# Two projections of the second block begun together, token-major, with seven held pieces

## The chip, the core and the metric

The kernel runs on one core of one Trainium2 chip. The time is the device time of one execution in microseconds. Five engines work in parallel, each through its own queue in order: TensorE (PE; its weight loads are shown as PEld), VectorE (DVE), ScalarE (ACT), GpSimd (POOL) and SyncE (SP), which issues the DMA transfers.

## The reference

Two transformer blocks on 256 tokens of width 1024 in float32. The first block (pool mixer, stick-breaking attention, cross-attention, dense feed-forward) is left as it is. The second one, cut to what matters:

```python
h = rms_norm(x, g_mix)
qa, ka, va, qb, kb, vb, qi, ki, wi, ga, gb = jnp.split(h @ w_in, SPLIT_POINTS, axis=-1)
qa = rope(heads(qa)); ka = rope(heads(ka)); qb = rope(heads(qb)); kb = rope(heads(kb))
qi = rope(qi.reshape(b, s, IDX_HEADS, IDX_DIM)); ki = rope(ki); wi = wi * IDX_SCALE
o_a = moba_attend(qa, ka, va)
o_b = dsa_attend(qb, kb, vb, qi, ki, wi)     # keys chosen by index scores:
#   score = einsum('qh,qhs->qs', wi, relu(einsum('qhd,sd->qhs', qi, ki)));  top 64 of them
mixed = sigmoid(ga) * (o_a @ w_proj_a) + sigmoid(gb) * (o_b @ w_proj_b)
x = x + mixed @ w_out
x = x + hier_moe(rms_norm(x, g_ffn), ...)    # 32 experts, two for each token
return rms_norm(x, g_final)
```

## The kernel before

A float32 product is made of three passes. `split_to` (L153) writes a high part with an ACT copy (whi, xhi; L155) and a low part with a subtraction on DVE, or on POOL where told so (wlo, xlo; L156). `mm3` (L185 to L187) then multiplies high by high, low by high and high by low into one accumulator.

Weights come by `wload` (L147) in chunks of 1 MB on SP's queue. A `piece` (L164) is half a chunk, split, 2 k-tiles of 512 columns. Its home is taken in turn from `homes`: for the projections discussed here either the usual pool (`base`, three buffers) or the pool `px2` (three buffers for each part). A projection of 512 columns has four pieces; for each token tile (two tiles of 128 tokens) a piece gives 6 matmuls of 512 columns, so a projection has 48. `ts_pair` (L219) forms pieces and multiplies each with token tile 0 and then 1; with `hold=4` it collects four pieces and then does all of tile 0 before tile 1.

The second block begins where the dense feed-forward ends. For each token tile `post_norm_add` (L305) adds the normalized feed-forward output to x (L312, L315), and `normed_T` (L285) normalizes x: ACT sums the squares (sqscr, L272), DVE adds them (rsm, L282), POOL takes the power (rsr, L284), DVE multiplies (ntok: L290 by the gain, L294 by rsr, L296 for the second half), PE transposes (xtp, L301), and the result is split to xhi and xlo. Tile 1 runs through this while PE already multiplies tile 0.

The first projection is qiT, the queries of the index scores, with four held pieces (L662), two of its low parts on POOL. `rope_heads` (L644) rotates a projection for each tile: three DVE products (L637, L638, L640; rr and r), an addition on POOL (L642), four transposes on PE (rt, L656) and a copy by ACT. After it come the index keys and weights (kiwi, 72 columns), the index scores (il, L702; DVE adds them up, L707), and on DVE the top-k of them (L712, L713), 16 steps. Then the projections qTb, kTb, vb of the attention "b" that uses that top-k, and qTa, kTa, va of "a". `attend` (L720) makes scores (as, L732), a masked maximum (L739), the exponentials on ACT (L746), the normalization (L752), the transposes of the probabilities (L756) and their product with v (ao, L765) to oah, oal, obh, obl. Last come gates (256-column matmuls, ACT's tanh into tg), the products y of the attention outputs (`merge`, L492; 24 matmuls each; DVE multiplies tg by y, L508), wo, the routing, and from L1117 the experts, whose weights (8 chunks of room) stream from HBM.

The order of the instructions on each engine isn't that of the code: a scheduler sets it when the program is built, within the pools' buffers and dependences. `issue_after` holds a split behind another one.

```python
qiT = rope_heads(3072, 1.0, "qiT", at, 4, first[0], 2, (1,3))
...
for name, c0, pool in (("b", 1536, atb), ("a", 0, at)):
    qT = rope_heads(c0, 0.125, "qT" + name, pool)
```

Of the kernel before, what the change touches and what calls it, by code (L numbers as in the profile page):

```python
# [9 lines left out]
F32 = mybir.dt.float32  # L10
# [8 lines left out]
P = 128  # L19
S = 256  # L20
D = 1024
NT = S // P
# [59 lines left out]
def block_kernel(ctx: ExitStack, tc: tile.TileContext, A, out: bass.AP):  # L82
    nc = tc.nc
# [134 lines left out]
    def ts_mm(dst, pcs, act, tt):  # L218
        for k0, per, pc in pcs:  # L219
            for j in range(per):  # L220
                mm3(dst, cut(act, k0 + j, tt), (pc[0][:, j, :], pc[1][:, j, :]), k0 + j == 0, k0 + j == KT - 1)

    def ts_pair(src, c0, n, act, name, hold=1, after=(), free=0, aside=()):
        o = acc_tile(name)
        kk = 2048 // n
        per = kk // 2
        group, npc, made = [], KT // per, 0
        for c in range(KT // kk):
            w = wload(rows(src, c * kk * P, kk, c0, n), kk, n)
            for h in range(2):  # L230
                group.append((c * kk + h * per, per, piece(w[:, h * per:(h + 1) * per, :], per, n,
                                                           after if made >= free else (),
                                                           nc.gpsimd if made in aside else None)))
                made += 1
                if len(group) == hold or made == npc:
                    for tt in range(NT):
                        ts_mm(o[tt][:, :n], group, act, tt)
                    group = []
                    hold = 1
        return o  # L240
# [375 lines left out]
    tmp = s2.enter_context(tc.tile_pool(name="at2t", bufs=2, side="right", reuse_waits="tile"))  # L616
    s1 = ExitStack()
    px = s1.enter_context(tc.tile_pool(name="px2", bufs=1, side="left", reuse_waits="tile"))
    homes.update(list=[base, (px, 3)], i=0)
    slots_of.update(list=[(ring, 4)], i=0)  # L620
    g_pre = gain_row(A["g_mix_2"][0])
    xt = xt_tiles()
# [18 lines left out]
                                in1=stab[:, tt, None, 32:64].to_broadcast([P, nh, 32]), op=ALU.mult)  # L641
        nc.gpsimd.tensor_tensor(out=dst, in0=t1, in1=t2, op=ALU.add)  # L642

    def rope_heads(c0, scale, name, pool, *how):  # L644
        o = ts_pair(w2in, c0, 512, xt, name, *how)
        if how:
            nc.sync.dma_start(out=cs2[:, 0:256], in_=A["c2"][:, 384:640])
            nc.sync.dma_start(out=cneg, in_=A["c2"][:, 0:384])
        dst = pool.tile([P, 4, S], F32, name=name, tag="qk", bufs=2)
        for tt in range(NT):  # L650
            r = rop.tile([P, 8, 64], F32, name="rr", tag="rr")
            rope_to(r, o[tt].rearrange("p (h d) -> p h d", h=8), tt, 8)
            b = m_tile("rt")
            rf = r.rearrange("p h d -> p (h d)")
            for c in range(4):
                nc.tensor.transpose(b[:, c * P:(c + 1) * P], rf[:, c * P:(c + 1) * P], ident)  # L656
            nc.scalar.activation(dst[:, :, tt * P:(tt + 1) * P], b.rearrange("p (c t) -> p c t", c=4), AF.Copy,
                                 scale=scale)
        return dst


    qiT = rope_heads(3072, 1.0, "qiT", at, 4, first[0], 2, (1,3))  # L662
    s1.close()
    homes.update(list=[base], i=0)
    s1 = ExitStack()
# [31 lines left out]
    def index_scores():  # L697
        for h in range(8):
            ks = slice((h % 2) * 64, (h % 2) * 64 + 64)
            b = m_tile("il")  # L700
            for tt, a0, a1 in SPANS:
                nc.tensor.matmul(b[:, a0:a1], lhsT=qiT[ks, h // 2, tt * P:(tt + 1) * P], rhs=kiT[ks, 0:a1 - a0],  # L702
                                 start=True, stop=True, skip_group_check=True)
            r = tmp.tile([P, 384], F32, name="irl", tag="ap", bufs=4)
            nc.scalar.activation(r, b[:, :384], AF.Relu)
            for tt, a0, a1 in SPANS:
                nc.vector.scalar_tensor_tensor(out=score[:, a0:a1], in0=r[:, a0:a1], scalar=wi[:, tt, h:h + 1],  # L707
                                               in1=(cneg if h == 0 else score)[:, a0:a1], op0=ALU.mult, op1=ALU.add)
        for tt, a0, a1 in SPANS:
            for _ in range(TOPK // 8):  # L710
                m8 = tmp.tile([P, 8], F32, name="m8", tag="m8")
                nc.vector.max(out=m8, in_=score[:, a0:a1])  # L712
                nc.vector.match_replace(out=score[:, a0:a1], in_to_replace=m8, in_values=score[:, a0:a1],  # L713
                                        imm_value=GONE)
        nc.vector.tensor_scalar(out=sbias, in0=score, scalar1=-2.9e38, scalar2=NEG, op0=ALU.is_gt, op1=ALU.mult)
        nc.vector.tensor_tensor(out=sbias, in0=sbias, in1=cneg, op=ALU.add)

    index_scores()

    def attend(qT, kT, v, bias, name):  # L720
# [48 lines left out]

    qkv = {}  # L770
    for name, c0, pool in (("b", 1536, atb), ("a", 0, at)):
        qT = rope_heads(c0, 0.125, "qT" + name, pool)
        kT = rope_heads(c0 + 512, 1.0, "kT" + name, pool)
        o = ts_pair(w2in, c0 + 1024, 512, xt, "v" + name)
        v = pool.tile([P, NT, 512], F32, name="v" + name)
        for tt in range(NT):
            nc.vector.tensor_copy(v[:, tt, :], o[tt])
        qkv[name] = (qT, kT, v)
# [457 lines left out]
```

## Time and profile before

| | us |
|---|---|
| runs | 1096.18, 1099.05, 1097.20 |
| median | 1097.2 |
| the profiled execution's time | 1095.6 |
| its span | 1093.9 |
| around the span | 1.7 |
| PE busy | 946.4 (87%) |
| DVE busy | 447.5 (41%) |
| ACT busy | 354.4 (32%) |
| POOL busy | 52.9 (5%) |

Mean granted clock of TensorE: 0.931. The span is the profiled execution from first to last instruction; the profiled time is the whole execution's. In a timeline a row gives the start, the duration, engine, line, operation and in brackets how long the engine had been idle before and what released it. Matmuls overlap, so a row's duration is longer than the distance between two starts.

### The profile page before, as it was taken

The numbers are of one execution on the slowest core, as the hardware profiler recorded it, in microseconds if no ns is written. First come the engines' busy times: TensorE is split into PE (matmuls) and PEld (weight loads), VectorE is DVE, ScalarE is ACT, GpSimd is POOL, SyncE is SP. The second block draws the span as 40 slices with busy tenths as digits, with TensorE's granted clock in tenths as the row PEclk, the third lists the DMA queues.
The fourth block names the chain that finished last, engine by engine and source line by source line (L and its number), as shares of the span: only waits on it lengthen the run. The fifth ranks groups of instructions, "written<-read, shape, count | busy, mean of one in ns | idle before, by whom it ended". The sixth has DMA issues, their size and how long they took to land.

```text
span 1093.9 us, 14757 instructions
## 1 busy us (share of the span) xinstructions
PE 946.4 (87%) x6119; PEld 653.5 (60%) x6119; DVE 447.5 (41%) x750; ACT 354.4 (32%) x552; POOL 52.9 (5%) x45
## 2 busy tenths in 40 slices
PE   6999999999999998999999999775776767667665
PEld 5989988978899996878889974222121212112101
DVE  5555536666545556679664751110101000011102
ACT  4555655555444444444655431000000000000002
POOL 1000012120000002211000000000000000000000
PEclk9999999999999999999999999887888877887879
DMA  9844347567555533645546789999999999999996
GB/s 330 276 157 155 116 135 251 194 238 262 191 192 190 165 101 112 228 153 181 166 171 238 305 302 420 419 419 422 416 421 417 418 416 421 418 419 420 417 422 269
DMA packets 109800, 310.76 MB, mean 284 GB/s; under 512 B 11040, under 2 KB 58144, under 8 KB 89376
## 3 DMA queue, kind: packets, MB, share of 16 engines
q1 hardware_dynamic: 109728, 309.77, 74.8%
q8 instruction: 49, 0.80, 0.3%
q14 instruction: 23, 0.19, 0.0%
HBM read 308.70 MB, written 1.05 MB: 283 GB/s over the span
## 4 chain that ended last, share of the span: by engine, by line
PE 57%; DMA 37%; DVE 3%; ACT 1%; issue 1%; SPq 1%; POOL 0%; POOLq 0%; ACTq 0%; DVEq 0%
DMA wchunk<-in_experts_dram 36%; PE gate L185 4%; PE gu L186 4%; PE gu L185 4%; PE gu L187 4%; PE gate L187 4%; PE gate L186 4%; PE hb L1117 2%; PE fo L185 2%; PE fo L187 2%; PE fo L186 2%; PE y L185 1%; PE y L187 1%; PE y L186 1%; PE wo L185 1%; PE wo L186 1%
## 5 line engine op out<-in xcount | busy, mean ns | idle before, releaser
L156 DVE TENSOR_TENSOR wlo<-wchunk,whi 128x1024 fp32r<-128x1024 f32 (+1 forms) x180 | 222.9, 1240 | 157.3 <-ACT whi L155 154.7
L155 ACT ACTIVATE whi<-wchunk 128x1024 fp32r<-128x1024 f32 (+1 forms) x193 | 200.8, 1048 | 223.7 <-PE gu L186 55.8
L1117 PE MATMUL hb<-wchunk,xs 128*32 128x512 f32 x1016 | 162.6, 739 | 80.5 <-DMA wchunk<-in_experts_dram 75.1
L1117 PEld LDWEIGHTS hb<-wchunk,xs 128*32 128x32 f32 x1016 | 25.9, 120 | 198.4 <-DMA wchunk<-in_experts_dram 156.4
L1117 PE MATMUL yb<-wchunk,mw 128*32 128x512 f32 (+1 forms) x544 | 71.6, 639 | 24.5 <-DMA wchunk<-in_experts_dram 21.8
L185 PE MATMUL gate<-xhi,whi 128*128 128x256 f32 x320 | 92.1, 288 | 0.6 <-DVE tg L508 0.6
L186 PE MATMUL gate<-xlo,whi 128*128 128x256 f32 x320 | 91.5, 286 | 0.0
L187 PE MATMUL gate<-xhi,wlo 128*128 128x256 f32 x320 | 91.4, 286 | 0.0
L187 PE MATMUL gu<-xhi,wlo 128*128 128x256 f32 x288 | 81.4, 283 | 0.0
L186 PE MATMUL gu<-xlo,whi 128*128 128x256 f32 x288 | 81.2, 282 | 0.0
L185 PE MATMUL gu<-xhi,whi 128*128 128x256 f32 x288 | 81.2, 282 | 0.0
L1181 DVE TENSOR_TENSOR x<-x,comb 128x512 f32<-128x512 f32 (+1 forms) x34 | 22.3, 656 | 126.6 <-PE comb L1179 126.6
L185 PEld LDWEIGHTS gate<-xhi,whi 128*128 128x128 f32 x320 | 61.2, 191 | 3.3 <-issue 2.4
L186 PEld LDWEIGHTS gate<-xlo,whi 128*128 128x128 f32 x320 | 61.2, 191 | 1.4 <-issue 1.3
L187 PEld LDWEIGHTS gate<-xhi,wlo 128*128 128x128 f32 x320 | 61.1, 191 | 1.4 <-issue 1.4
L1117 PEld LDWEIGHTS yb<-wchunk,mw 128*32 128x32 f32 x544 | 14.3, 117 | 76.5 <-DMA wchunk<-in_experts_dram 46.5
L1144 ACT ACTIVATE mw<-hT 128x512 f32<-128x512 f32 x8 | 4.8, 597 | 167.4 <-PE hT L1142 167.4
L987 DVE TENSOR_TENSOR xs<-gat,gk 128x512 f32<-128x512 f32 x16 | 11.1, 692 | 115.7 <-PE gat L979 115.7
L185 PEld LDWEIGHTS gu<-xhi,whi 128*128 128x128 f32 x288 | 55.1, 191 | 0.3
L186 PEld LDWEIGHTS gu<-xlo,whi 128*128 128x128 f32 x288 | 54.9, 191 | 0.3
L187 PEld LDWEIGHTS gu<-xhi,wlo 128*128 128x128 f32 x288 | 54.8, 190 | 0.0
L1139 DVE TENSOR_TENSOR mw<-hb,ms 128x512 f32<-128x512 f32 x8 | 5.5, 692 | 106.2 <-PE hb L1117 106.2
(395 smaller groups left out, 1687.8 us busy)
## 6 DMA issues: line engine op xcount, KB each, us to landing
wchunk<-in_experts_dram SPq DMA_DIRECT2D x187, 1024.0 KB, 19.9
wchunk<-in_w_in_dram SPq DMA_DIRECT2D x43, 1024.0 KB, 5.3
wchunk<-in_w_ffn_in_dram SPq DMA_DIRECT2D x22, 1024.0 KB, 5.2
wchunk<-in_w_ffn_out_dram SPq DMA_DIRECT2D x11, 1024.0 KB, 5.0
wchunk<-in_w_out_dram SPq DMA_DIRECT2D x8, 1024.0 KB, 5.8
wchunk<-in_experts_dram SPq DMA_DIRECT2D x8, 512.0 KB, 14.4
wchunk<-in_w_mem_kv_dram SPq DMA_DIRECT2D x2, 1024.0 KB, 6.8
wchunk<-in_w_pool_o_dram SPq DMA_DIRECT2D x2, 1024.0 KB, 5.3
```

The costliest lines, as they stand in the source:

```text
L155: a = nc.scalar.activation(hi, src, AF.Copy)
L156: return a, (eng or nc.vector).tensor_tensor(out=lo, in0=src, in1=hi.bitcast(F32), op=ALU.subtract)
L185: nc.tensor.matmul(o, lhsT=lh[0], rhs=rh[0], start=start, stop=False)
L186: nc.tensor.matmul(o, lhsT=lh[0], rhs=rh[1], start=False, stop=False)
L187: return nc.tensor.matmul(o, lhsT=lh[1], rhs=rh[0], start=False, stop=stop)
L987: nc.vector.tensor_tensor(out=xss[g][:, ks, :], in0=b.rearrange("p (k t) -> p k t", k=4), in1=gk[:, ks, None].to_broadcast([P, 4, P]), op= ...
L1117: nc.tensor.matmul(o[ps, :].rearrange("p (h n) -> p h n", h=m), lhsT=lhsT[:, ps], rhs=w[e], start=first, stop=last, skip_group_check=True, ...
L1139: nc.vector.tensor_tensor(out=h, in0=hb[1], in1=s, op=ALU.mult)
L1144: nc.scalar.activation(mw[:, 1, :], b, AF.Copy)
L1181: nc.vector.tensor_tensor(out=xa, in0=xa, in1=cb[:, :n], op=ALU.add)
```

## The change

qiT and qTb are projected together. Their eight pieces are formed up front; qiT's four and three of qTb's are held (seven), for which px2 gets a fourth buffer. Token tile 0 is multiplied with qiT's pieces and three of qTb's, then tile 1 with qiT's, then the fourth of qTb's with tile 0 and all of them with tile 1. The rope of qiT follows, that of qTb stands before the index scores; the loop over "b" and "a" takes this qTb.

```diff
--- before.py
+++ after.py
@@ -616,7 +616,7 @@
     tmp = s2.enter_context(tc.tile_pool(name="at2t", bufs=2, side="right", reuse_waits="tile"))
     s1 = ExitStack()
     px = s1.enter_context(tc.tile_pool(name="px2", bufs=1, side="left", reuse_waits="tile"))
-    homes.update(list=[base, (px, 3)], i=0)
+    homes.update(list=[base, (px, 4)], i=0)
     slots_of.update(list=[(ring, 4)], i=0)
     g_pre = gain_row(A["g_mix_2"][0])
     xt = xt_tiles()
@@ -641,11 +641,8 @@
                                 in1=stab[:, tt, None, 32:64].to_broadcast([P, nh, 32]), op=ALU.mult)
         nc.gpsimd.tensor_tensor(out=dst, in0=t1, in1=t2, op=ALU.add)
 
-    def rope_heads(c0, scale, name, pool, *how):
-        o = ts_pair(w2in, c0, 512, xt, name, *how)
-        if how:
-            nc.sync.dma_start(out=cs2[:, 0:256], in_=A["c2"][:, 384:640])
-            nc.sync.dma_start(out=cneg, in_=A["c2"][:, 0:384])
+    def rope_heads(c0, scale, name, pool, o=None):
+        o = o or ts_pair(w2in, c0, 512, xt, name)
         dst = pool.tile([P, 4, S], F32, name=name, tag="qk", bufs=2)
         for tt in range(NT):
             r = rop.tile([P, 8, 64], F32, name="rr", tag="rr")
@@ -659,7 +656,20 @@
         return dst
 
 
-    qiT = rope_heads(3072, 1.0, "qiT", at, 4, first[0], 2, (1,3))
+    qp = ts_pieces(w2in, 3072, 512, first[0], 2, (1, 3))
+    bp = ts_pieces(w2in, 1536, 512, first[0], 0, ())
+    nc.sync.dma_start(out=cs2[:, 0:256], in_=A["c2"][:, 384:640])
+    nc.sync.dma_start(out=cneg, in_=A["c2"][:, 0:384])
+    qo, bo = {}, {}
+    for tt in range(NT):
+        for o, n in ((qo, "qiT"), (bo, "qTb")):
+            o[tt] = acc1.tile([P, 512], F32, name=n, tag="acc", bufs=4)
+        ts_mm(qo[tt], qp, xt, tt)
+        if tt == 0:
+            ts_mm(bo[0], bp[:3], xt, 0)
+    ts_mm(bo[0], bp[3:], xt, 0)
+    ts_mm(bo[1], bp, xt, 1)
+    qiT = rope_heads(3072, 1.0, "qiT", at, qo)
     s1.close()
     homes.update(list=[base], i=0)
     s1 = ExitStack()
@@ -715,6 +725,7 @@
         nc.vector.tensor_scalar(out=sbias, in0=score, scalar1=-2.9e38, scalar2=NEG, op0=ALU.is_gt, op1=ALU.mult)
         nc.vector.tensor_tensor(out=sbias, in0=sbias, in1=cneg, op=ALU.add)
 
+    qTb = rope_heads(1536, 0.125, "qTb", atb, bo)
     index_scores()
 
     def attend(qT, kT, v, bias, name):
@@ -769,7 +780,7 @@
 
     qkv = {}
     for name, c0, pool in (("b", 1536, atb), ("a", 0, at)):
-        qT = rope_heads(c0, 0.125, "qT" + name, pool)
+        qT = qTb if name == "b" else rope_heads(c0, 0.125, "qT" + name, pool)
         kT = rope_heads(c0 + 512, 1.0, "kT" + name, pool)
         o = ts_pair(w2in, c0 + 1024, 512, xt, "v" + name)
         v = pool.tile([P, NT, 512], F32, name="v" + name)
```

The new order of the instructions around the second norm, with buffer numbers. On PE, at the end of tile 0 (qiT's first accumulator is 4117 before and 4157 now, its second 4118 and 4201; qTb's are 4158 and 4202), before:

```order
L185 MATMUL qiT_4117<-whi_4134,xhi_4031 128x512
L186 MATMUL qiT_4117<-wlo_4135,xhi_4031 128x512
L187 MATMUL qiT_4117<-whi_4134,xlo_4032 128x512
L301 MATMUL xtp_4100<-ck_86,ntok_4088 128x128 x4
L301 MATMUL xtp_4108<-ck_86,ntok_4088 128x128 x4
L185 MATMUL qiT_4118<-whi_4121,xhi_4031 128x512
L186 MATMUL qiT_4118<-wlo_4122,xhi_4031 128x512
```

and now:

```order
L186 MATMUL qTb_4158<-wlo_4149,xhi_4031 128x512
L187 MATMUL qTb_4158<-whi_4148,xlo_4032 128x512
L185 MATMUL qTb_4158<-whi_4148,xhi_4031 128x512
L186 MATMUL qTb_4158<-wlo_4149,xhi_4031 128x512
L187 MATMUL qTb_4158<-whi_4148,xlo_4032 128x512
L301 MATMUL xtp_4100<-ck_86,ntok_4088 128x128 x4
L301 MATMUL xtp_4108<-ck_86,ntok_4088 128x128 x4
L185 MATMUL qiT_4201<-whi_4119,xhi_4031 128x512
L186 MATMUL qiT_4201<-wlo_4120,xhi_4031 128x512
L185 MATMUL qTb_4202<-whi_4138,xhi_4031 128x512
L186 MATMUL qTb_4202<-wlo_4139,xhi_4031 128x512
L187 MATMUL qiT_4201<-whi_4119,xlo_4032 128x512
```

Between qiT's last matmul of tile 0 and the transposes stand 18 matmuls of qTb now, of which the last are shown, and the first low pass (L187) of tile 1 comes after two of qTb's.

On DVE, from the residual addition of tile 1 (L315) on, before:

```order
L315 SCALAR_TENSOR_TENSOR x<-pn,rsr,x 128x512 x2
L290 TENSOR_TENSOR ntok<-x,grow 128x512
L282 TENSOR_SCALAR rsm<-ss 128x1
L294 TENSOR_SCALAR ntok<-ntok,rsr 128x512
L296 SCALAR_TENSOR_TENSOR ntok<-x,rsr,grow 128x512
L637 TENSOR_TENSOR rr<-qiT,cs_4116 128x512
L638 TENSOR_TENSOR r_4190<-qiT,cs_4116 128x8x32
L640 TENSOR_TENSOR r_4190<-qiT,cs_4116 128x8x32
```

and now:

```order
L315 SCALAR_TENSOR_TENSOR x<-pn,rsr,x 128x512 x2
L156 TENSOR_TENSOR wlo<-wchunk,whi 128x1024
L290 TENSOR_TENSOR ntok<-x,grow 128x512
L156 TENSOR_TENSOR wlo<-wchunk,whi 128x1024 x2
L637 TENSOR_TENSOR rr<-qiT,cs_4116 128x512
L638 TENSOR_TENSOR r_4259<-qiT,cs_4116 128x8x32
L640 TENSOR_TENSOR r_4259<-qiT,cs_4116 128x8x32
L282 TENSOR_SCALAR rsm<-ss 128x1
L294 TENSOR_SCALAR ntok<-ntok,rsr 128x512
L296 SCALAR_TENSOR_TENSOR ntok<-x,rsr,grow 128x512
```

Three weight splits and the rope of qiT's tile 0 (L637 to L640) moved ahead of rsm; L294 and L296, before the rope until now, come after it.

On POOL, in the same place, before:

```order
L284 TENSOR_TENSOR rsr<-rsm,half 128x1
L156 TENSOR_TENSOR wlo<-wchunk,whi 128x1024
L284 TENSOR_TENSOR rsr<-rsm,half 128x1
L642 TENSOR_TENSOR rr<-rr,r_4190 128x512
L642 TENSOR_TENSOR rr<-rr,r_4202 128x512
```

and now:

```order
L284 TENSOR_TENSOR rsr<-rsm,half 128x1
L156 TENSOR_TENSOR wlo<-wchunk,whi 128x1024
L642 TENSOR_TENSOR rr<-rr,r_4259 128x512
L284 TENSOR_TENSOR rsr<-rsm,half 128x1
L642 TENSOR_TENSOR rr<-rr,r_4271 128x512
```

The rope's addition (L642) went ahead of rsr (L284) of the second tile.

On PE at the end of the gates (y_5773 before is the first y; now y_5804 and y_5774 are under way together with the last product ao of attention "a"), the semaphore waits written behind the rows, before:

```order
L186 MATMUL y_5802<-obl_4903,whi_5799 128x256
L187 MATMUL y_5802<-obh_4902,wlo_5770 128x256
L185 MATMUL y_5835<-oah_5076,whi_5831 128x256 [waits DVE_49]
L186 MATMUL y_5835<-oal_5077,whi_5831 128x256
L187 MATMUL y_5835<-oah_5076,wlo_5832 128x256
```

and now:

```order
L776 MATMUL ao_5245<-apts_5243,va_4901 64x128
L186 MATMUL y_5804<-obl_4905,whi_5800 128x256
L187 MATMUL y_5804<-obh_4904,wlo_5801 128x256
L185 MATMUL y_5774<-oah_5078,whi_5771 128x256 [waits Activation_49]
L185 MATMUL y_5836<-oah_5078,whi_5833 128x256 [waits DVE_49]
L186 MATMUL y_5836<-oal_5079,whi_5833 128x256
```

The y that waits for DVE now stands one matmul behind the end of y_5804; before, y_5835 with the same kind of wait stood one whole y (y_5802) behind the end of y_5773.

## Rows read from the trace of the kernel before

**Rows 1.** The chain in order of time, 640 to 700 us: start us, us, what

```profile
652.53 13.87 PE hb L1117 x128
...
682.36 20.09 DMA wchunk<-in_experts_dram
```

**Rows 2.** Busy time by stretch: PE, PEld, DVE, ACT, POOL, granted clock, DMA share, GB/s

```profile
640.00:650.00 10.00, 9.27 (x80) 8.62 (x79) 6.81 (x45) 6.38 (x15) 1.09 (x2) 1.00 0.94 352
650.00:660.00 10.00, 10.00 (x95) 4.67 (x97) 2.41 (x10) 0.36 (x1) 0.00 (x0) 1.00 0.67 251
```

**Rows 3.** The chain in order of time: one 512-column and one 256-column matmul

```profile
438.29 0.23 PE qiT L186
...
590.20 0.12 PE gate L187
```

**Rows 4.** Timeline of PE, 432 to 438 us: start, us, engine, line, operation

```profile
432.48 0.40 PE L187 MATMUL qiT<-whi,xlo 128*128 128x512 f32 x1
435.13 1.29 PE L301 MATMUL xtp<-ck,ntok 128*128 128x128 f32 x8 [2.25 <-DVE ntok L294]
436.45 0.50 PE L185 MATMUL qiT<-whi,xhi 128*128 128x512 f32 x1
436.78 0.40 PE L186 MATMUL qiT<-wlo,xhi 128*128 128x512 f32 x1
437.56 0.50 PE L187 MATMUL qiT<-whi,xlo 128*128 128x512 f32 x1 [0.39 <-DVE xlo L156]
```

**Rows 5.** Timeline of DVE, 427 to 437 us

```profile
427.90 1.24 DVE L156 TENSOR_TENSOR wlo<-wchunk,whi 128x1024 fp32r<-128x1024 f32 x1
429.07 3.54 DVE L315 SCALAR_TENSOR_TENSOR x<-pn,rsr,x 128x512 f32<-128x512 f32 x2
432.53 0.68 DVE L290 TENSOR_TENSOR ntok<-x,grow 128x512 f32<-128x512 f32 x1
433.56 0.21 DVE L282 TENSOR_SCALAR rsm<-ss 128x1 f32<-128x1 f32 x1 [0.34 <-ACT sqscr L272]
434.50 0.49 DVE L294 TENSOR_SCALAR ntok<-ntok,rsr 128x512 f32<-128x512 f32 x1 [0.73 <-POOL rsr L284]
...
435.56 0.68 DVE L637 TENSOR_TENSOR rr<-qiT,cs 128x512 f32<-128x512 f32 x1
...
436.83 1.28 DVE L156 TENSOR_TENSOR xlo<-xtp,xhi 128x512 fp32r<-128x512 f32 x2
```

**Rows 6.** Timeline of DVE: the same addition for token tile 0

```profile
418.63 1.42 DVE L315 SCALAR_TENSOR_TENSOR x<-pn,rsr,x 128x512 f32<-128x512 f32 x2
```

**Rows 7.** Timeline of POOL, 428 to 437 us and 499 us

```profile
428.90 2.50 POOL L156 TENSOR_TENSOR wlo<-wchunk,whi 128x1024 fp32r<-128x1024 f32 x1 [0.47 <-ACT whi L155]
433.92 0.55 POOL L284 TENSOR_TENSOR rsr<-rsm,half 128x1 f32<-128x1 f32 x1 [2.52 <-DVE rsm L282]
436.99 1.28 POOL L642 TENSOR_TENSOR rr<-rr,r 128x512 f32<-128x512 f32 x1 [2.52 <-DVE r L640]
...
499.36 1.30 POOL L642 TENSOR_TENSOR rr<-rr,r 128x512 f32<-128x512 f32 x1 [0.22 <-DVE r L640]
```

**Rows 8.** Timeline of DVE, from the first top-k step to the first softmax

```profile
482.86 0.29 DVE L712 MAX8 m<-score 128x8 f32<-128x128 f32 x1
...
499.63 2.11 DVE L156 TENSOR_TENSOR wlo<-wchunk,whi 128x1024 fp32r<-128x1024 f32 x1
...
519.95 0.29 DVE L739 CUSTOM_DVE_ANT_0 ap<-as,score 128x128 f32<-128x128 f32 x1 [0.15 <-DVE score L716]
...
524.20 1.01 DVE L752 TENSOR_SCALAR ap<-ap,arc 128x128 f32<-128x128 f32 x4
```

**Rows 9.** Timeline of PE: the first transposes of probabilities

```profile
527.21 0.33 PE L756 MATMUL as<-ck,ap 128*128 128x128 f32 x1
```

**Rows 10.** Timeline of PE and of DVE: the end of the first y

```profile
598.67 0.28 PE L187 MATMUL y<-oah,wlo 128*128 128x256 f32 x1
...
599.00 0.69 DVE L508 SCALAR_TENSOR_TENSOR tg<-tg,y 128x512 f32<-128x512 f32 x1 [0.69 <-PE y L187]
```

## The prediction

> **What bounds the kernel now.** I read the chain of the work that ended last first, in order of time: it is on PE up to 682.36 us and then runs in 20-us steps of expert loads nearly to the end [rows 1]. That DMA stage does not hide what is lost before it. In 640 to 650 us the DMA engines are 0.94 busy and in 650 to 660 only 0.67, since all expert slots are full and the queue waits for the first expert matmul (hb, at 652.53 us) to free them [rows 1, 2]. So a microsecond by which PE reaches hb sooner or later moves the slots, the loads behind them and the end by a microsecond. I price the change on PE's time up to 652 us, one to one.
>
> From the start of the second block's projections (426 us) to 640 us PE is packed: a 512-column matmul starts every 0.23 us, a 256-column one every 0.12 [rows 3]. There are two openings where the change works [rows 4]. After the last qiT matmul of token tile 0 (432.48 us) the transposes of tile 1's normalized tokens come only at 435.13, with 2.25 us idle, released by the ntok write of VectorE. And the first L187 of tile 1 waits 0.39 us more for xlo. Counted by starts these are 435.13 - 432.48 - 0.23 = 2.42 us and (437.56 - 436.78) - 0.23 = 0.55 us. Together 2.97 us is all that more work in this place can win. The measurement of this kernel can tell about 0.3%, 3.3 us, from no change; the full gain would be below that.
>
> **Why tile 1's tokens are late.** On DVE the residual add L315 takes 3.54 us for two halves, 429.07 to 432.61, where the same pair for tile 0 took 1.42 [rows 5, 6]; a 2.50-us weight split runs on POOL from 428.90 to 431.40 [rows 7]. Then L290 (432.53), ScalarE's sums of squares, rsm (433.56), POOL's power rsr (433.92 for 0.55) and L294 (434.50), whose end releases PE. Neither that POOL split nor the add is touched, so I take x ready at 432.6 again.
>
> **Part 1, the fill: 18 matmuls more before the transposes.** Three held pieces of qTb, 6 matmuls each, stand between qiT's tile 0 and xtp: 18 x 0.23 = 4.1 us of work done earlier that is missing later. No matmul is added or dropped by the change, so PE's total is unmoved.
>
> **Part 2, what comes with the fill: splits and a rope ahead of the norm.** The three pieces need three wlo on DVE, and the new order puts all three and the rope of qiT's tile 0 (L637 to L640) between the residual add and rsm. A split took 1.24 us, 1.17 from its start to the next start; the rope runs from 435.56 to the next start at 436.83, 1.27 us; L290's 0.68 overlaps with the next by as much, so 0.60 [rows 5]. So rsm starts at 432.53 + 3 x 1.17 + 0.60 + 1.27 = 437.9 us instead of 433.56. In the new order POOL then has the rope's add (1.28 us) ahead of rsr, where it had rsr first. The add starts when L640 ends, about 438.0, and ends at 439.3. Then rsr, and L294 0.58 us after its start as before (433.92 to 434.50): 439.9 instead of 434.50, 5.4 us later [rows 5, 7]. The first matmul of tile 1 follows L294 by 1.95 us (436.45) [rows 4], so it stands at 441.85. PE has 4.1 us of work in these 5.4: a loss of 1.3 us. The waiting in all grows: PE waits for the lows of the first two qTb pieces (some 0.9 and 0.4 us) and 2.5 us for ntok.
>
> The second wait goes: in the new order two qTb matmuls stand between tile 1's first two and its first L187, and the rope that held DVE before xlo has already run. That wins 0.5 of the 0.55. **Part 1 and 2 together: +0.8 us**, between -2.97 (both openings filled, nothing new late) and +1.3 (the loss and no gain at xlo). I stay near the upper end since the queues run in order: rsm cannot pass the splits and the rope, rsr cannot pass the add.
>
> The further loads cost nothing: the two qTb chunks take the two places in SP's queue that the small index-key chunk and the first qTb chunk had, ahead of the norm; what slips back is wanted after qTb. One more px2 buffer costs only room. ScalarE's three more hi splits stand ahead of the squares of x, which cannot start before the residual add has made x, at 432 us in any case. Of the table loads cs and cneg only the place in the code changes.
>
> **Part 3, the index scores come later.** By the new order 239 instead of 179 512-column matmuls stand, from qiT's first, before the last index score matmul, and 8 transposes more: 60 x 0.23 + 0.8 = 14.6 us later. The top-k, which began at 482.86 [rows 8], begins at about 497.5. It held DVE 37.1 us, to the first softmax step at 519.95. In the new order two splits and two ropes fewer lie in it: 37.1 - 2 x 1.17 - 2 x 1.27 = 32.2, so 529.7. The first normalized probabilities were there 5.3 us after (524.20 + 1.01), so at 535. PE transposed them at 527.21 [rows 9]. In the new order 124 gate matmuls stand before that transpose, before 25: 99 x 0.12 = 11.9 us of cover. PE comes at 527.21 + 11.9 + 0.8 = 539.9. The cover outlasts the delay by some 5 us, or 3 if one or two gate splits hold DVE in between. **Part 3: 0**, bounded by 0 and, without cover, one us for each us later than 539.9.
>
> Inside the top-k a split took 2.11 us at 499.63 instead of 1.21 to 1.24, while POOL's rope add ran from 499.36 for 1.30 [rows 7, 8]. The Trainium skill (SBUF — State Buffer, "SBUF: two separate sides") says that VectorE and GpSimd share a port pair as an exclusive lock, which a DVE instruction with two SBUF inputs takes only against a GpSimd instruction that reads SBUF, and that the loser is blocked entirely. The trace agrees, by 0.9 us at 499.63 and by 2.1 us at the residual add. By that rule the two adds that leave the top-k would spare up to 1.8 us more; the sum goes by plain durations.
>
> **Part 4, the end of the gates.** In the old order a whole y of 24 matmuls (2.9 us) stands between a y's last matmul and the next that needs its PSUM buffer. In the new order y_5836 starts one matmul after y_5804's last and waits for DVE to have read it. Before, L508 started 0.33 us after the start of y's last matmul and took 0.69 (598.67 to 599.69) [rows 10]: 1.02 us, less the 0.24 that PE has to do, is 0.8 us of idle. Next y_5866 waits for its wlo, which DVE does after that L508 and others; I take 0.6 (0 for a split done in time, 1.2 for a whole one). **Part 4: +1.4 us**, 0 to 2.0.
>
> **Sum:** 0.8 + 0 + 1.4 = +2.2 us. The profiled execution took 1095.6 us; with the change 1097.8. The median of the runs shown is 1.6 above the profiled one (1097.2), so the forecast is 1099.4 us.
>
> **Rivals.**
> - *The fill does what the gap asks for.* If rsm and rsr do not stand behind splits and rope, or these end before ScalarE's sums, both openings go: -2.97 and no tail waits, 1094.2 us. For it: DVE has idle stretches of 0.34 and 0.73 us in the gap [rows 5]. Against it: the order of both queues. Chance 0.15.
> - *The softmax comes uncovered.* DVE's queue through the top-k holds the splits of the gates that are to cover it; a split waits for its hi, and what stands behind on DVE waits too. If top-k takes the old 37.1 us, the probabilities are there at 540, at PE's arrival, and nothing is lost yet; that is the point from which it decides. Three blocked splits (0.9 us each) beyond it cost 2.7 us: 1102.1. For it: DVE did not idle in the old top-k, and POOL's adds blocked it. Against it: five us of margin. Chance 0.20, the slower side.
> - *The tail waits are not there*, since DVE reads y in time or PE is later there: +0.8 only, 1098.0 us. Chance 0.20.
> - The change's own effect at the first transposes cannot fail to come: the order has the seven pieces there.
>
> **How the numbers follow.** The forecast, 1099.4, holds 0.45; it spreads over 1098.5 to 1101 by the bounds of parts 2 and 4. Faster by over 0.3% means below 1093.9: only part of the first rival, 0.05. Slower means above 1100.5: most of the second rival and the upper part of the forecast, 0.17 + 0.13 = 0.30. Within 0.3%: 0.65. The range 1094.6 to 1103 leaves out the better half of the first rival and the worst of the second.
>
> **What would show it.** Right: in the new trace the add of POOL stands before rsr, tile 1's transposes start near 440.5 and its first qiT matmul near 441.9; the wait before xtp is still over 2 us; no PE wait at the first probabilities near 540; one wait of PE for L508 near 600; hb near 654.7. Wrong: xtp before 438 us (first rival), a PE wait of some us for ap (second), or hb earlier than 652.5, which would say that something outside these places was won.

## The result, and the profile after

The changed kernel takes 1106.4 us (median of 4 runs, 1105.99 to 1108.86), the kernel before 1097.9 in the same comparison (1096.18 to 1099.05): the ratio is 1.0086, with an interval of 1.0074 to 1.0098. By the medians it is slower by 8.5 us, nearly four times the 2.2 us that were forecast, and outside the range. Its profiled execution took 1105.99 us, with a span of 1104.3.

The last chain has the shape of [rows 1], later. The chain of work that ended last, changed kernel (start us, us, what):

```profile
662.44 13.87 PE hb L1128 x128
...
695.22 20.00 DMA wchunk<-in_experts_dram
```

The first expert matmuls stand at 662.44 instead of 652.53. The start of the second block itself moves from one execution to the next (the first qiT matmul stood at 426.5 to 430.6 us in the profiles of this case), so from here on I count from that matmul to hb: 652.53 - 426.49 = 226.0 us before, 662.44 - 427.04 = 235.4 now. Nearly all that was lost lies between them.

The place that the change was made at. Timeline of PE, changed kernel, from qTb's first low pass to tile 1 of qiT:

```profile
434.40 0.50 PE L186 MATMUL qTb<-wlo,xhi 128*128 128x512 f32 x1 [0.83 <-DVE wlo L156]
...
438.55 0.39 PE L187 MATMUL qTb<-whi,xlo 128*128 128x512 f32 x1
...
441.06 1.46 PE L301 MATMUL xtp<-ck,ntok 128*128 128x128 f32 x8 [2.12 <-DVE ntok L294]
442.38 0.79 PE L185 MATMUL qiT<-whi,xhi 128*128 128x512 f32 x1
442.97 0.63 PE L186 MATMUL qiT<-wlo,xhi 128*128 128x512 f32 x1
443.40 0.63 PE L185 MATMUL qTb<-whi,xhi 128*128 128x512 f32 x1
...
445.51 0.39 PE L187 MATMUL qiT<-whi,xlo 128*128 128x512 f32 x1
445.73 0.39 PE L185 MATMUL qiT<-whi,xhi 128*128 128x512 f32 x1
```

Against [rows 4]: the opening of 2.25 us is filled with 18 matmuls and has opened again behind them, 2.12 us for the same ntok, with another 0.83 us for a weight's low part inside the fill. No wait for xlo is left. And from 442.4 to 445.5 the matmuls start 0.43 us apart instead of 0.23.

The queues that hold ntok, in the timelines of DVE and then of POOL, changed kernel:

```profile
433.13 1.21 DVE L156 TENSOR_TENSOR wlo<-wchunk,whi 128x1024 fp32r<-128x1024 f32 x1
434.27 0.68 DVE L290 TENSOR_TENSOR ntok<-x,grow 128x512 f32<-128x512 f32 x1
434.87 2.35 DVE L156 TENSOR_TENSOR wlo<-wchunk,whi 128x1024 fp32r<-128x1024 f32 x2
437.14 0.68 DVE L637 TENSOR_TENSOR rr<-qiT,cs 128x512 f32<-128x512 f32 x1
...
438.40 0.20 DVE L282 TENSOR_SCALAR rsm<-ss 128x1 f32<-128x1 f32 x1
440.43 0.49 DVE L294 TENSOR_SCALAR ntok<-ntok,rsr 128x512 f32<-128x512 f32 x1 [1.83 <-POOL rsr L284]
...
438.62 1.26 POOL L642 TENSOR_TENSOR rr<-rr,r 128x512 f32<-128x512 f32 x1 [6.63 <-DVE rsm L282]
439.85 0.55 POOL L284 TENSOR_TENSOR rsr<-rsm,half 128x1 f32<-128x1 f32 x1
```

Against [rows 5, 7]: three splits and the rope run between x and rsm, and the rope's addition ahead of rsr. L294 follows the first qiT matmul by 13.4 us instead of 8.0, 5.4 us later.

Why the matmuls were slow: busy time by stretch of 2 us, changed kernel (PE, PEld, DVE, ACT, POOL, granted clock, DMA share, GB/s):

```profile
440.00:442.00 2.00, 0.91 (x7) 0.73 (x8) 1.15 (x2) 0.27 (x1) 0.39 (x1) 1.00 0.24 91
442.00:444.00 2.00, 2.00 (x8) 1.46 (x7) 1.38 (x2) 0.92 (x2) 0.00 (x0) 0.51 0.57 172
444.00:446.00 2.00, 2.00 (x8) 1.56 (x7) 0.00 (x0) 0.07 (x1) 0.00 (x0) 0.63 1.03 434
```

The granted clock, 0.51 of 2.4 GHz, is at its lower level, 1.2 GHz, for some 3 us after the idle stretch.

Then a place that the prediction passed over: the index scores. A visit of PE to them, in the kernel before (timeline of PE):

```profile
463.27 0.61 PE L185 MATMUL kTb<-whi,xhi 128*128 128x512 f32 x2
463.81 0.93 PE L702 MATMUL il<-kiT,qiT 64*128 64x128 f32 x8
464.68 0.50 PE L186 MATMUL kTb<-wlo,xhi 128*128 128x512 f32 x1
465.01 0.39 PE L187 MATMUL kTb<-whi,xlo 128*128 128x512 f32 x1
```

and in the changed one:

```profile
479.69 0.39 PE L185 MATMUL vb<-whi,xhi 128*128 128x512 f32 x1
480.01 0.92 PE L712 MATMUL il<-kiT,qiT 64*128 64x128 f32 x4
480.86 0.50 PE L186 MATMUL vb<-wlo,xhi 128*128 128x512 f32 x1
481.19 0.39 PE L187 MATMUL vb<-whi,xlo 128*128 128x512 f32 x1
```

Before, PE goes there 4 times for two heads (8 matmuls; each matmul of the code stands in the trace as two); now 8 times for one head (4 matmuls). Four take as long as eight: 0.85 us to the next matmul's start against 0.87. The neighbours add to each visit: 0.32 us to it and 0.33 after it where 0.23 is usual, 0.19 together. Eight visits cost 8 x 1.04 = 8.3 us, four 4 x 1.06 = 4.2: **4.1 us more for the same 32 matmuls.**

Last, the end of the gates, timelines of PE and of DVE, changed kernel:

```profile
607.17 0.39 PE L185 MATMUL y<-obh,whi 128*128 128x256 f32 x1
607.48 0.86 PE L776 MATMUL ao<-apts,va 128*64 128x256 f32 x6
608.27 0.39 PE L186 MATMUL y<-obl,whi 128*128 128x256 f32 x1
608.50 0.28 PE L187 MATMUL y<-obh,wlo 128*128 128x256 f32 x1
608.82 0.39 PE L185 MATMUL y<-oah,whi 128*128 128x256 f32 x1
609.56 0.38 PE L185 MATMUL y<-oah,whi 128*128 128x256 f32 x1 [0.35 <-DVE tg L508]
...
608.82 0.69 DVE L508 SCALAR_TENSOR_TENSOR tg<-tg,y 128x512 f32<-128x512 f32 x1 [4.20 <-PE y L187]
```

One y waits for L508 as the order said; 0.74 us lie between two starts where 0.12 is usual, 0.62 us. The y's lose elsewhere too, where they change places with other matmuls: 0.31 us lie behind the y matmul that stands alone between two groups of ao (607.17). Summed from each start to the next, the 192 y matmuls take 24.8 us instead of 23.0, **1.8 us more**, of which that wait is a third.

### The profile page after: what moved, and what is told of

Same layout as the page of the kernel before. It is cut to its first block, busy times and chain, and to the rows that moved or that the text cites. A ratio compares the mean times of both kernels' runs of the same rounds, so it can differ in the third digit from the quotient of the medians.

```text
span 1104.3 us, 14758 instructions
## 1 busy us (share of the span) xinstructions
PE 959.4 (87%) x6119; PEld 658.2 (60%) x6119; DVE 447.3 (41%) x750; ACT 353.1 (32%) x552; POOL 56.5 (5%) x45
## 4 chain that ended last, share of the span: by engine, by line
PE 59%; DMA 35%; DVE 3%; ACT 1%; issue 1%; SPq 1%; POOL 0%; POOLq 0%; DVEq 0%; ACTq 0%
DMA wchunk<-in_experts_dram 33%; PE gate L185 4%; PE gu L186 4%; PE gu L185 4%; PE gu L187 4%; PE gate L186 4%; PE gate L187 4%; PE hb L1128 3%; PE fo L185 2%; PE fo L187 2%; PE fo L186 2%; PE y L185 1%; PE gat L990 1%; PE y L187 1%; PE y L186 1%; PE wo L185 1%
## 5 line engine op out<-in xcount | busy, mean ns | idle before, releaser
L156 DVE TENSOR_TENSOR wlo<-wchunk,whi 128x1024 fp32r<-128x1024 f32 x180 | 222.4, 1238 | 153.5 <-ACT whi L155 151.3
L187 PE MATMUL gate<-xhi,wlo 128*128 128x256 f32 x320 | 91.4, 286 | 0.0
L187 PE MATMUL gu<-xhi,wlo 128*128 128x256 f32 x288 | 81.3, 282 | 0.0
L187 PEld LDWEIGHTS gate<-xhi,wlo 128*128 128x128 f32 x320 | 61.0, 191 | 0.8 <-issue 0.8
L187 PEld LDWEIGHTS gu<-xhi,wlo 128*128 128x128 f32 x288 | 54.8, 190 | 0.0
```

The source lines that it names most:

```text
L156: return a, (eng or nc.vector).tensor_tensor(out=lo, in0=src, in1=hi.bitcast(F32), op=ALU.subtract)
L187: return nc.tensor.matmul(o, lhsT=lh[1], rhs=rh[0], start=False, stop=stop)
```

## The experiments

The theory after the traces (theory A): three things make the loss. The norm stands behind splits and rope, and the clock may fall after the idle stretch; lone heads cost PE as much as pairs; the attention and the gates' end suffer from what comes later. The rival was the second one of the prediction in a wider form, that the late top-k alone is to blame.

**1. The norm ahead of the rope.** Changed kernel, with

```diff
-            rope_to(r, o[tt].rearrange("p (h d) -> p h d", h=8), tt, 8)
+            with ExitStack() as q:
+                for ins in after:
+                    q.enter_context(tc.issue_after(ins.ins))
+                rope_to(r, o[tt].rearrange("p (h d) -> p h d", h=8), tt, 8)
...
-    qiT = rope_heads(3072, 1.0, "qiT", at, qo)
+    qiT = rope_heads(3072, 1.0, "qiT", at, qo, first[1])
```

> The changed kernel with one edge more: the rope of qiT's tile 0 may be issued on VectorE only after the second tile's normalization, so that POOL has the power rsr ahead of the rope's addition again. The three weight splits stay ahead of the norm. Theory A (the queues ahead of the norm, and the clock that falls after the idle stretch, are part of the loss): L294 comes 1.27 + 1.28 = 2.5 us earlier, at about 437.9; PE ends the 18 matmuls of the fill at about the same time, so the 2.12 us of idle before the transposes go, the granted clock stays at 1.00 there and the 1.4 us that eight slow matmuls and transposes cost are not lost: about 3.5 us less than the changed kernel, 1102.9 us. Theory B (only the late index scores and what follows from them count, the wait is made good later): within 1 us of the changed kernel, 1106. Theory C (the clock falls for another reason than the idle stretch): the wait goes and the clock falls nevertheless, 2.1 us less, 1104.3.

Measured: 1102.5 us, ratio to before 1.0046 (1.0033 to 1.0059), 3.9 us less than the changed kernel. Timeline of PE around the transposes and of POOL, this kernel:

```profile
438.75 0.40 PE L187 MATMUL qTb<-whi,xlo 128*128 128x512 f32 x1
438.99 1.20 PE L301 MATMUL xtp<-ck,ntok 128*128 128x128 f32 x8
440.27 0.50 PE L185 MATMUL qiT<-whi,xhi 128*128 128x512 f32 x1
...
437.68 0.55 POOL L284 TENSOR_TENSOR rsr<-rsm,half 128x1 f32<-128x1 f32 x1 [5.49 <-DVE rsm L282]
```

No idle before the transposes, and the granted clock is 1.00 in every stretch around them. From the first qiT matmul to hb it takes 231.7 us. So the wait at the norm was real, and it came from the two queues. One wait of 0.85 us for a weight's low part is left inside the fill.

**2. qTb's rope behind the index scores in the code again.**

```diff
-    qTb = rope_heads(1536, 0.125, "qTb", atb, bo)
     index_scores()
+    qTb = rope_heads(1536, 0.125, "qTb", atb, bo)
```

> The changed kernel with one part undone: qTb's rope stands behind the index scores in the code again. By the new order the index score matmuls then run for two heads together, in 4 visits of 8 matmuls, where the changed kernel has 8 visits of 4; the first of them stands at nearly the same place. Theory A (a head alone costs PE as much as two together, 0.85 us a visit, since two 64-row matmuls run side by side): 4 visits less at 0.85 and about 0.2 for the switches, some 4.2 us less than the changed kernel, 1102.2 us. Theory B (the loss is the late top-k and what it does to the attention): the top-k still begins some 14 us later than before the change, so no gain, 1106.

Measured: 1103.7 us, ratio 1.0053 (1.0040 to 1.0066), 2.7 us less than the changed kernel. The visits to the index scores are 4 again, 3.5 us in all instead of 6.8. That it is 2.7 and not 4.2 has its own row, in the timeline of PE, this kernel:

```profile
502.41 0.50 PE L185 MATMUL kTa<-whi,xhi 128*128 128x512 f32 x1 [1.38 <-DVE r L640]
```

PE waits for a rope of DVE, which stands in the queue behind the first top-k steps. The wait is new; neither theory had it. It isn't the whole account: by the sums from start to start the y's are back at 23.0 us, which wins 1.8, and the attention's scores and the transposes of probabilities cost 1.2 more than in the changed kernel. So 2.7 us is a balance of several terms and not the price of the heads alone.

**3. Both edits together.**

> Both edits of the changed kernel together: the norm ahead of qiT's rope, and qTb's rope behind the index scores in the code. Theory A: the two terms add, 3.5 + 4.2 = 7.7 us less than the changed kernel, 1098.7 us, near the kernel before; what is left over it is the attention's and the gates' end, some 2 to 4 us, less the filled opening of 2.4 us. Theory B: at most 1 us less, 1105.5.

Measured: 1099.4 us, ratio 1.0021 (1.0012 to 1.0031), 7.0 us less than the changed kernel; the two edits alone gave 3.9 and 2.7, together 6.6. They add. The same wait of 1.38 us is in this trace too.

**4. The kernel before, with the heads taken apart.**

```diff
+        prev = None
...
+                if prev is not None:
+                    tc.add_manual_dep(prev.ins, m.ins.name, mybir.DependencyInfo(mybir.DependencyClass.NoSync,
+                                      mybir.DependencyReason.DATA), reason="one head at a time")
...
-            nc.scalar.activation(r, b[:, :384], AF.Relu)
+            prev = nc.scalar.activation(r, b[:, :384], AF.Relu)
```

> The kernel before the change with one edit: an edge lets a head's index score matmuls be ordered only behind the activation of the head before it. By the order they then run in 7 visits (the first still with two heads) instead of 4. Nothing is moved ahead of the norm. Theory A: 3 visits more at 0.85 us and 0.2 for the switches, 3.2 us more than before, 1101.1 us. Theory B (a single head costs half of two): 3 x 0.2 = 0.6 us more, 1098.5, and the visits are 0.45 us long.

Measured: 1101.7 us, ratio 1.0038 (1.0025 to 1.0050), 3.9 us more than before. Timeline of PE, this kernel:

```profile
477.66 0.92 PE L703 MATMUL il<-kiT,qiT 64*128 64x128 f32 x4
...
478.93 0.92 PE L703 MATMUL il<-kiT,qiT 64*128 64x128 f32 x4
```

A lone head lasts 0.85 us in this kernel as well, not 0.45. Nothing was moved ahead of the norm here, and the last visit to the index scores starts some 4 us later (485.4 - 427.5 = 57.9 us after the first qiT matmul instead of 53.5), which the changed kernel exceeds by far (74.4). The seven visits (the first still for two heads) and their neighbours take 3.1 us more than the four of before, where theory A had 3.2. The rest of the 3.9 is no price of these heads: the order changed further on too, and the attention's scores and transposes cost 1.5 us more, other matmuls some 0.6 less. Its profile also shows the clock's fall that experiment 7 is about: from the first qiT matmul to hb 231.3 us, less 1.4 for the fall 229.9, 3.9 more than the kernel before without a fall.

**5. The changed kernel with the heads in pairs.** The rope keeps its place; only the matmuls of two heads are chained in turn:

```diff
+                for j in range(2):
+                    ks = slice(j * 64, j * 64 + 64)
+                    with ExitStack() as q:
+                        if last is not None:
+                            q.enter_context(tc.issue_after(last.ins))
+                        last = nc.tensor.matmul(bs[j][:, a0:a1], lhsT=qiT[ks, hp, tt * P:(tt + 1) * P],
+                                                rhs=kiT[ks, 0:a1 - a0], start=True, stop=True, skip_group_check=True)
```

> The changed kernel with the index score matmuls of two heads chained in turn (span 1 of both heads, then span 2 of both), nothing else: qTb's rope keeps its place in the code and the norm stays late. By the order they run in 5 visits instead of 8 (the first pair is cut into 1 and 3). Theory A (a lone head costs PE as much as two): from 6.80 us for all visits to some 0.4 + 0.85 + 3 x 0.87 = 3.9, and three switches of 0.18 less: 3.4 us less than the changed kernel, 1103 us. Theory B (the gain of the kernel with the late rope came from the rope's place and not from the pairs): no gain, 1106.

Measured: 1099.9 us, ratio 1.0019 (1.0010 to 1.0028), 6.5 us less than the changed kernel, 3.1 more than theory A gave to it. The index scores took what was expected, 3.8 us in 5 visits. Timeline of PE, this kernel, the pair that is cut in two:

```profile
479.93 0.48 PE L716 MATMUL il<-kiT,qiT 64*128 64x128 f32 x2
...
482.61 0.92 PE L716 MATMUL il<-kiT,qiT 64*128 64x128 f32 x6
```

The other gain lies behind them: no y waits for DVE in this trace, and the order of the attention and of the gates' end is another one. From the first qiT matmul to hb this profile has 229.8 us, 5.6 less than the changed kernel's 235.4 (the clock fell in both, see experiment 7); the visits and their neighbours make 3.6 of it, and the y's, 23.2 us instead of 24.8, make 1.6. The last visit starts 72.4 us after the first qiT matmul, in the changed kernel 74.4: the top-k is nearly as late, and most of the loss is gone. So the rival falls with this run and the one before it: the scores' matmuls themselves cost the time, though part of what follows them went with them.

**6. The score matmuls of the attentions in pairs.** Kernel of experiment 3, with the same chain over the two heads of a pair in `attend`.

```diff
-            for j in range(2):
-                ks = slice(j * 64, j * 64 + 64)
-                for tt, a0, a1 in SPANS:
-                    nc.tensor.matmul(sc[j][:, a0:a1], lhsT=qT[ks, hp, tt * P:(tt + 1) * P],
+            for tt, a0, a1 in SPANS:
+                for j in range(2):
+                    ks = slice(j * 64, j * 64 + 64)
...
+                        last = nc.tensor.matmul(sc[j][:, a0:a1], lhsT=qT[ks, hp, tt * P:(tt + 1) * P],
```

> The kernel with the norm first and the rope late, and in both attentions the score matmuls of a head pair chained in turn, so that by the order 7 of the 8 pairs run as 1 and 3 instructions instead of 2 and 2. Theory A (two instructions of one head last as long as three of which two are of different heads): a pair costs 0.42 + 0.85 instead of 0.85 + 0.85; the visits go from 12.5 to about 10.6 us, so 1.9 us less than without the edit, 1097.5 us. Theory B: the scores' matmuls are covered by what they wait for, no gain, 1099.4.

Measured: 1097.2 us, ratio 0.9995 (0.9985 to 1.0005), 2.3 us less than without it. A pair's scores in the timeline of PE, kernel of experiment 3:

```profile
554.78 0.92 PE L746 MATMUL as<-kTa,qTa 64*128 64x128 f32 x4
...
558.02 0.92 PE L746 MATMUL as<-kTa,qTa 64*128 64x128 f32 x4
```

and in this one:

```profile
554.92 0.48 PE L750 MATMUL as<-kTa,qTa 64*128 64x128 f32 x2
...
558.48 0.92 PE L750 MATMUL as<-kTa,qTa 64*128 64x128 f32 x6
```

Two and six instead of four and four: 0.42 + 0.85 us to the next start instead of 0.85 twice. It is the same price at another place: all visits take 10.3 us instead of 12.5. The wait of 1.38 us of experiment 2 is still in this trace. This kernel has the change with its norm, its heads and its attention mended, and it is as fast as the one before, not faster.

**7. Does the clock fall by chance?** Second and third profiles of the kernel before and a second one of the changed kernel.

> The kernel before the change again, for a second profile. Theory A (whether the clock falls after the 2.25 us of idle is left to chance): the idle stretch before the transposes is again 2.25 us; the granted clock in the 6 us after it is either 1.00 or has a stretch near 0.50 that costs 1 to 1.5 us, as in the kernel with the heads apart, which is the same up to there. Theory C (that kernel's fall had another cause): 1.00 again in every look.

> The kernel before the change once more, for a third profile: the same two outcomes as the second look; with chance at work one of the two looks shows the fall.

> The changed kernel again, for a second profile. Theory A: 0.83 and 2.12 us of idle before the transposes again, and after them the clock at about 0.50 for some 3 us, since it fell in both kernels with this order; if it stays at 1.00 here, the time is 1.3 us shorter and the fall is left to chance with 2.1 us of idle too.

Measured: the clock fell in the second profile of the kernel before, not in the third, and not in the second profile of the changed kernel. Busy time by stretch, second profile of the kernel before (its idle stretch of 2.25 us ends at 438.54):

```profile
440.00:442.00 2.00, 1.65 (x5) 0.99 (x6) 1.51 (x3) 0.46 (x1) 1.27 (x1) 0.60 0.96 270
442.00:444.00 2.00, 2.00 (x7) 1.57 (x6) 0.21 (x1) 0.68 (x1) 0.00 (x0) 0.54 1.00 422
```

Second profile of the changed kernel (idle for 0.82 and 2.12 us, up to 441.09):

```profile
442.00:444.00 2.00, 1.98 (x11) 1.48 (x10) 1.36 (x2) 0.95 (x2) 0.00 (x0) 1.00 0.65 164
444.00:446.00 2.00, 2.00 (x11) 1.65 (x10) 0.36 (x1) 1.10 (x2) 0.00 (x0) 1.00 1.03 434
```

From the first qiT matmul to hb the kernel before took 226.0, 227.4 (clock fell) and 226.1 us; the changed one 235.4 (fell) and 234.0. A fall costs about 1.4 us in either. Compared like with like the change costs 234.0 - 226.0 = 8.0 us, or 235.4 - 227.4 = 8.0. The profiles of experiments 2, 4 and 5, whose opening is as long, show a fall too. In all, the clock fell in 2 of 4 profiles after 2.25 or 2.26 us of idle (the kernel before and experiment 4) and in 3 of 4 after 2.12 to 2.16 us with the wait inside the fill ahead of it (the changed kernel, experiments 2 and 5). So few profiles can't tell whether the change makes a fall likelier; the 8.0 us hold without it. This corrects theory A on the clock, and the account of experiment 1 with it: up to 1.4 of its 3.9 us may come from a fall that its kernel no longer risks, and the profiles without a fall differ by 2.3 us (234.0 and 231.7). With the opening filled (experiments 1, 3, 6 and 8) no profile shows a fall.

**8. A version that fills the opening with what needs no VectorE.** Of two of qTb's pieces only the high part is made early:

```diff
-    bp = ts_pieces(w2in, 1536, 512, first[0], 0, ())
+    bw = [wload(rows(w2in, c * 512, 4, 1536, 512), 4, 512) for c in range(2)]
+    bv = [bw[i // 2][:, (i % 2) * 2:(i % 2) * 2 + 2, :] for i in range(4)]
+    bp = [(2 * i, 2, half_piece(bv[i])) for i in range(2)]
...
+    ts_mm(qo[0], qp, xt, 0)
+    ts_pass(bo[0], bp, 0, ((0, 0), (1, 0)), True)
+    ts_mm(qo[1], qp, xt, 1)
+    qiT = rope_heads(3072, 1.0, "qiT", at, qo, first[1])
...
-    pc = piece(w, KT, 72)
+    pc = piece(w, KT, 72, first[1])
...
+    for i in range(2):
+        with tc.issue_after(first[1][1].ins):
+            nc.vector.tensor_tensor(out=bp[i][2][1], in0=bv[i], in1=bp[i][2][0].bitcast(F32), op=ALU.subtract)
+    ts_pass(bo[0], bp, 0, ((0, 1),))
...
     index_scores()
+    qTb = rope_heads(1536, 0.125, "qTb", atb, bo)
```

`half_piece` makes the high part alone on ACT; `ts_pass` runs single passes of the three, named by which part of the tokens and of the weights they take.

> A version that fills the opening without new work for VectorE ahead of the norm: of two of qTb's pieces only the high part (ScalarE) is made early, and the two passes that need only it (high by high, low tokens by high weights) run ahead of the transposes, 8 matmuls; their low parts, the rope of qiT and the low part of the small index-key piece are issued on VectorE after the second norm; the index keys come before the rest of qTb, and qTb's rope stands behind the index scores. By the order the index scores run in 4 visits and VectorE's row from the residual addition to xlo is that of the kernel before. Theory A: the transposes stay at the place of before (8.6 us after the first qiT matmul), 8 x 0.23 = 1.8 us of the 2.4 us opening are filled, what PE idles is under 0.7 us and the clock stays at 1.00; the rest as before: 1.8 to 2.4 us less than before, 1095.4 to 1096. Theory B (what is moved ahead of the index keys costs more than it fills): the same as before or slower, 1097.8 to 1101.

Measured: 1094.7 us, ratio 0.9973 (0.9963 to 0.9983): 2.7 us faster than before, faster than both kernels. Timeline of PE around the transposes, this kernel:

```profile
434.57 0.39 PE L187 MATMUL qiT<-whi,xlo 128*128 128x512 f32 x1
435.59 1.29 PE L301 MATMUL xtp<-ck,ntok 128*128 128x128 f32 x8 [0.63 <-DVE ntok L294]
436.91 0.50 PE L185 MATMUL qiT<-whi,xhi 128*128 128x512 f32 x1
```

Its chain that ended last:

```profile
650.40 13.87 PE hb L1153 x128
```

The transposes stand 8.65 us after the first qiT matmul, as before (8.64); 0.63 us of idle are left of 2.25, and hb comes after 223.5 us instead of 226.0. That is a little more than theory A's 1.8 to 2.4 us. With the index keys left at their place, the visits to the index scores and to the attention's scores are those of the kernel before.

## Why the prediction was wrong

**What bounds the kernel** was right: hb moved by what PE lost, and the time with it (span +10.4 us, of it 9.4 from the first qiT matmul to hb, 0.55 ahead of that and 0.5 behind).

**Parts 1 and 2 (+0.8 us)** were right in the mechanism and in most rows. From the first qiT matmul to the first of tile 1 it took 436.45 - 426.49 = 9.96 us, now 442.38 - 427.04 = 15.34: 5.38 us more, 5.4 forecast, for 4.1 us of work; the wait for xlo went. The wait before xtp was forecast as 2.5 us and was 2.12. All matmuls of qiT and qTb together cost 0.4 us more (table below), half of the forecast. The clock was not in the sum; it fell in this profile and costs 1.4 us, but does so in some executions of before as well.

**Part 3 (0)** held for the wait that it looked for and failed for what it left out. The top-k began at 503.6 us (forecast 497.5), the first softmax step came at 537.5 (529.7), the first transposes of probabilities at 546.5 (539.9), and PE did not wait for them. Of the six us by which the top-k came later than forecast, 4.1 are the lone heads below and 1.4 the clock's fall. Timelines of DVE and of PE, changed kernel:

```profile
503.63 0.29 DVE L722 MAX8 m<-score 128x8 f32<-128x128 f32 x1
...
537.47 0.29 DVE L750 CUSTOM_DVE_ANT_0 ap<-as,score 128x128 f32<-128x128 f32 x1
...
546.55 0.27 PE L767 MATMUL as<-ck,ap 128*128 128x128 f32 x1
```

The step that failed is the price of the index scores, put at nothing by a sentence of part 1: "No matmul is added or dropped by the change, so PE's total is unmoved." The same matmuls cost PE more in other company. The order showed the index score heads one at a time, and I counted what stands before them instead of pricing how they stand. That is 4.1 us by the visits of PE; experiments 4 and 5 show the price in two other kernels. The same price at the attention's scores makes 1.3 us more (all visits 12.1 us instead of 10.8, summed from start to next start); experiment 6 shows that this price is paid in full: 2.2 us less in the visits, 2.3 us less in the time.

**Part 4 (+1.4 us)** came out in size, 1.8 us and within its bounds, but partly by luck: the wait for L508 is there, 0.62 us by starts for 0.8 forecast; the wait for a wlo, forecast as 0.6, is under 0.2. The other 1.0 us, which the prediction did not have, is again a matter of company: in nine places, next to a transpose, to ao or to the other y or right behind a wait, 0.2 to 0.3 us pass after a y's matmul instead of 0.12. In experiments 2, 3 and 6, where the y's run whole, they take 23.0 us as before. No run changed the order of the y's alone.

The sum as measured, without the clock: each matmul's time from its start to the next start, from the first qiT matmul to hb, in the first profile of the kernel before and the second of the changed kernel (no fall in either):

| matmuls | before, us | changed, us | more |
|---|---|---|---|
| qiT, qTb (parts 1 and 2) | 25.95 | 26.36 | +0.4 |
| il, the index scores | 3.45 | 6.79 | +3.3 |
| kTb, vb, qTa, kTa, va (0.8 of it beside il) | 56.27 | 57.68 | +1.4 |
| as, the attention's scores | 10.80 | 12.07 | +1.3 |
| y | 23.04 | 24.83 | +1.8 |
| all others | 106.46 | 106.15 | -0.3 |
| sum | 225.97 | 233.88 | +7.9 |

So 0.4 + 4.1 + 1.3 + 1.8 = 7.6 of 7.9 us have their place. The 0.3 us left is a balance: 0.6 more in the projections away from il, 0.4 more in the gates and other matmuls, 0.7 less in the transposes. Why those moved was not tested.

**The rivals.** The fill that does what the gap asks for did not occur, for the reason given, and experiment 8 shows that it can be had for 2.7 us when nothing is put ahead of the norm on DVE. The uncovered softmax did not occur either; the cover held. The right side came out, by a mechanism that stood among none of them, and the range, built from the bounds of the places that I had priced, could not hold it.

## What to carry to other kernels

A change of order is priced by who stands next to whom, not only by what waits: count the visits of an engine to each kind of work in the new order, and take the price of a visit from the trace, for the shape of visit that will stand there. To fill an idle stretch, choose work that needs nothing from the engine whose result is awaited; here two of the three passes of a split product need of the weights only the high part, which ScalarE makes. And whatever is begun early pushes back what it is put ahead of. Experiment 8 kept the long chain behind it (here the index keys, top-k and softmax) at its place and was the fastest; what a late chain costs by itself no run shows, apart from the wait of 1.38 us in experiments 2, 3 and 6.

## What the runs showed of the hardware

Matmuls over 64 rows: four of one head take 0.85 us to the next start, eight of two heads, which sit on the two halves of the rows, 0.87. The two heads run side by side (in the visit at 463.81 us the second head's first matmul starts 0.01 us behind the first head's), and a lone one takes the same time for half the work. The Trainium skill (TensorE: Matmul & The Clock Gate, "Part 3: Packing small matmuls — row/col tiling") says that matmuls on different tiles of the array run concurrently. The trace agrees: 0.87 against 0.85 us.

After the same 2.25 us of idle, in the same program, the granted clock fell to 1.2 GHz in one execution and stayed at 2.4 in two others; a fall cost 1.4 us. A single profile can thus differ from the next by that much with no cause in the program, so compare two profiles only when both show a fall or neither does.
